# A fifth row buffer for gathered expert rows in the dense stage, and the Gelu of a dot issued a step later

## Chip, cores and metric

The kernel runs on one core of one Trainium2 chip. The metric is the device time of one execution in microseconds (us), median of the runs shown. Engines are named as the profile names them: PE (TensorE; PEld is its weight load), DVE (VectorE), ACT (ScalarE), POOL (GpSimd), SP (SyncE). POOL and SP do no arithmetic that matters here: they issue transfers.

## What is computed

The kernel is one layer of a hybrid network for 9 tiles of 128 tokens, each token a row of 1024 float32 values. A trunk (gated mixing, retention, projections) ends with scores for product-key retrieval. Each token then picks 8 heads x 16 = 128 experts out of 16384, and every expert is one row of `expert_u` and one of `expert_v`:

```python
experts = e1 * P_NKEYS + e2
w = jax.nn.softmax(vals, axis=-1).astype(t.dtype)
a = jax.nn.gelu(jnp.einsum('td,thkd->thk', t, eu[experts]))
return jnp.einsum('thk,thkd->td', w * a, ev[experts])
```

The result is added to the token's row and normalised.

## The kernel before, in words

**Two forms of the expert layer.** Token tiles 0, 1, 2, 6, 7 are *gathered*. For each of the 128 experts of a token, POOL issues one indirect transfer (L766) that brings, for the tile's 128 tokens, one row each of `euv` (2048 floats: u beside v, 128 x 8 KB = 1.05 MB) into a row buffer `gat`. DVE forms the dot of the u half with the token (L739, with a short read of its sum, `sdot`), ACT takes Gelu and multiplies by the softmax weight (L741, L742), and DVE adds the weighted v half to `acc` (L753). 5 x 128 = 640 such gathers are made. Tiles 3, 4, 5, 8 take the *dense* form: all 16384 experts in 128 steps of 128 experts. A step `e` forms `S` (24 matmuls, L988), ACT takes Gelu into `a` (L995), DVE multiplies by the spilled expert weights `pt` (L997), ACT and DVE split the product into two parts `g` (L200 cast, L204 subtract), and PE multiplies the parts with those of `ev` into `res` (18 matmuls) and `blk` (6 on average, L960), which DVE adds to `oacc` (L969).

**Weights of a dense step.** `fetch` (L937) loads 128 rows of u (`in_eud`) and of v (`in_evd`), 512 KB each, through four raw buffers `wraw`. `split_u` (L942) and `split_v` (L947) split them into two parts: an ACT cast (L200: `whi`, `ev`) and a DVE subtract (L204: `wlo`, `ev`). Every eighth step loads a 2 MB block of `pt`.

**Stages.** The trunk runs to about 2344 us with gathers beside it. Then comes the entry to the dense stage: the best keys and weights of tile 8 on DVE (L631 to L731), and their expansion into DRAM (`expand`, L772). The dense stage runs from 2494 to about 4111 us with the other gathers beside it, then the last norms.

**Order.** The program is written as generators: `advance` (L891) lets two lanes run, gathers and the preparation of expert weights, each yield counting modelled microseconds (a gather 5, one of a dense step's two halves 24 x 512 / 2400). A scheduler then places each engine's instructions by priority and by when it thinks their inputs are ready; dense work is issued at a raised priority (`DP`), and so is the preparation of the last tiles (`BOOST`). On the chip every engine takes its instructions in that fixed order, so an instruction that waits holds up all behind it on its engine.

**The pipeline of gathers** (L744): there are `GB = 4` row buffers. A gather is put on `queue`; the row issued `AHEAD = 2` steps ago is dotted and its Gelu issued at once; the row of the step before that is added, which frees its buffer. The transfer into a buffer can start when the add of the row four before is done.

```python
def gathered():
    if len(queue) > AHEAD and queue[AHEAD] is not None:
        dots(*queue[AHEAD])
    if len(queue) > AHEAD + LAG:
        last = queue.pop()
```

Of the kernel before, what the change touches and what calls it, by code (L numbers as in the profile page):

```python
# [17 lines left out]
P = 128  # L18
D = 1024
# [9 lines left out]

# units of the packed weights: [unit][128 rows of a k tile][4 k tiles][256 columns]  # L30
U_IN, U_PA, U_PB, U_OUT, U_Q, N_UNITS = 0, 80, 88, 104, 112, 128

# columns of the packed small vectors and constants
C_GMIX, C_GSGU, C_BG, C_GFFN, C_SK1, C_SK2 = 0, 8, 16, 32, 40, 168
N_VEC = 296
K_KDP, K_EPP, K_DMP, K_TRI, K_IOTA, K_ID = 0, 4, 8, 520, 648, 776
N_CST = 904
# the same for the sample tile
S_KDS, S_EPS, S_DMS, S_TRS = 0, 32, 36, 548
N_SMP = 676  # L40

GROUPS = [[0, 1], [2, 3, 4, 5], [6, 7, 8]]
# the token tiles whose experts' rows are gathered, and those that take the dense form
GATHER, DENSE = [0, 1, 2, 6, 7], [3, 4, 5, 8]
# those whose best keys are found next to the scores
EARLY = [0, 1, 8]
TD = len(DENSE) * P
EC = 4      # tokens in one product of their expert weights
LT = 16     # tokens in a run of the spilled expert weights
BE = 8      # second keys in one load of them  # L50

# [3 lines left out]
def step_kernel(ctx: ExitStack, tc: tile.TileContext, x, state, wall, wst, bs, rows, vec, cst, smp, cosd, sind, euv,  # L55
# [34 lines left out]

    # ---- weights: loaded ahead, split into two float32r parts whose sum is exact
    order = []
# [22 lines left out]
    def load(n):  # L115
        nonlocal pair
        if n < per - 2 and n % 3 < 2:
            # the slots of the gathered rows are free until the first token tiles are through
            if n % 3 == 0:
                pair = peer.tile([P, 2, 4, 256], F32, name="gat", bufs=GB)  # L120
            t = pair[:, n % 3]
        else:
            t = wp.tile([P, 4, 256], F32, name="wraw", bufs=NRAW)
        nc.sync.dma_start(t, wall[order[n]])
        return t

    def take():
        """the two parts of the weights of the next unit"""
        n = wst_["take"]
        wst_["take"] += 1  # L130
        while wst_["split"] < min(n + 3, len(order)):
            s = wst_["split"]
            while wst_["load"] < min(s + n_raw(wst_["load"]), len(order)):
                l = wst_["load"]
                raws[l] = load(l)
                wst_["load"] += 1
            hi, lo = (wp.tile([P, 4, 256], F32R, name=n, bufs=NPART) for n in ("whi", "wlo"))
            split((hi, lo), raws.pop(s))
            parts[s] = (hi, lo)
            wst_["split"] += 1  # L140
        return order[n], parts.pop(n)
# [6 lines left out]
    def store(out, src, after=2):  # L148
        """a store of something just computed: issued later, so that its wait holds up no load"""
        late.append([after, out, src])  # L150
# [11 lines left out]
    def col(t, k, T):  # L162
        """the k-th 128 rows of transposed activations: one tile, or one of every two"""
        return t[k // 2][:, k % 2, :T] if isinstance(t, list) else t[:, k, :T]

    def gemm_f(acts, T, base, nk=2):
        """columns of the weights on the partitions: [128, 2, T]"""
        ps = gp.tile([P, 2, 512], F32, name="gps")
# [12 lines left out]
    def gemm_t(acts, nt, base):  # L181
        """tokens on the partitions: [128, nt, 256]"""
        ps = gp.tile([P, 4, 256], F32, name="gps")
# [13 lines left out]
    def split(parts, src, scale=None):  # L197
        """parts[0] = float32r(src * scale), parts[1] = src * scale - parts[0]"""
        if scale is None:
            nc.scalar.copy(parts[0], src)  # L200
        else:
            nc.scalar.activation(parts[0], src, AF.Copy, scale=scale)
        if scale is None:
            nc.vector.tensor_tensor(parts[1], src, parts[0].bitcast(F32), op=OP.subtract)  # L204
        else:
            nc.vector.scalar_tensor_tensor(parts[1], src, scale, parts[0].bitcast(F32), op0=OP.mult, op1=OP.subtract)
# [11 lines left out]

    # ---- trunk of one group of token tiles, up to the sub-key scores
    hTs = {}  # L220

    def front(gi, pl):
        """the first norm of a group, transposed"""
        tl = GROUPS[gi]
# [217 lines left out]
    def gating(pl, tl, nt, T, sample, hT, pb):  # L442
        # of every two channel groups, the normalised v and then the high parts of their products
        va = []
# [94 lines left out]
    def project(pl, tl, nt, T, mT, tT, rs):  # L539
        """x + m @ w_out; the products with w_query start from it times g_ffn, their scores take the norm's factor"""  # L540
        grow = pl.tile([P, D], F32, name="grow")
# [74 lines left out]

    # ---- product-key retrieval
    AHEAD, LAG = 2, 1
    PACE = [5.0]
    BOOST = [100]  # L620
    AB = 2
    EUB, RWB = 3, 4
    AA = (1, 3)
# [15 lines left out]
    def top_keys(t, h, src):  # L639
        """the 16 best keys of each half of a head"""  # L640
        if t not in early:
# [10 lines left out]
    def topk_units(kind, t):  # L652
        """the experts of a token tile and their softmax weights"""
        d = T_[t] = {}
# [18 lines left out]
        v12, i12 = early.pop(t)  # L673
        # pairs (i, j) that may be among the 16 largest sums: (i + 1)(j + 1) <= 16, in the order of 16 i + j,
        # with a few more that make the rows regular
        cand = peer.tile([P, PH, 64], F32, name="cand", tag="oh")
# [59 lines left out]

    def dots(t, j, b):
        d = T_[t]
        nc.vector.tensor_tensor_reduce(out=b[:, :D], in0=b[:, :D], in1=d["x"], op0=OP.mult, op1=OP.add,  # L739
                                       scale=1.0, scalar=0.0, accum_out=d["s"][:, j:j + 1])  # L740
        nc.scalar.activation(d["s"][:, j:j + 1], d["s"][:, j:j + 1], AF.Gelu_apprx_tanh)  # L741
        nc.scalar.activation(d["s"][:, j:j + 1], d["s"][:, j:j + 1], AF.Copy, scale=d["w"][:, j:j + 1])  # L742

    def gathered():  # L744
        """one step of the pipeline gather -> dot -> accumulate"""
        if len(queue) > AHEAD and queue[AHEAD] is not None:
            dots(*queue[AHEAD])
        if len(queue) > AHEAD + LAG:
            last = queue.pop()
            if last is not None:  # L750
                t, j, b = last
                d = T_[t]
                nc.vector.scalar_tensor_tensor(d["acc"], b[:, D:], d["s"][:, j:j + 1], d["acc"], op0=OP.mult, op1=OP.add)  # L753
                if j == HK - 1:
                    out_norm(d["acc"], peer.tile([P, 2 * D], F32, name="gat", bufs=GB), t)
                    del T_[t]

    def gather(t):
# [5 lines left out]
        for j in range(HK):  # L764
            b = peer.tile([P, 2 * D], F32, name="gat", bufs=GB)
            nc.gpsimd.indirect_dma_start(out=b, out_offset=None, in_=euv,  # L766
# [5 lines left out]
    def expand(t):  # L772
        """the softmax weights of a token tile over all experts: [first key, second key, token], into DRAM"""
        d = T_.pop(t)
# [25 lines left out]
        for c in range(P // EC):  # L800
# [9 lines left out]
            for j in range(EC):  # L810
# [4 lines left out]
                else:  # L815
                    # max(0, w - w (n - e)^2) is w at n = e and 0 elsewhere
                    nc.scalar.activation(ab[:, 0, j], io, AF.Square, scale=-1.0, bias=eT[:, 0, k:k + 1])
# [8 lines left out]
    def out_norm(acc, tmp, t):  # L826
        """the last norm; tmp takes the squares and the norm's weights"""
        nc.sync.dma_start(tmp[:, D:], row_bcast(rows, 2))
        final_norm(acc, tmp[:, :D], tmp[:, D:], t)
# [10 lines left out]
    def prepare():  # L840
        """the top-k of all tiles, and the weights of the dense ones"""
        left, wait = list(GATHER), list(DENSE)
# [15 lines left out]
    def gather_all():  # L858
        for t in GATHER:
            while t not in staged:  # L860
                if any(queue):
                    queue.insert(0, None)
# [3 lines left out]
            yield from gather(t)  # L866
        for _ in range(AHEAD + LAG + 1):
            queue.insert(0, None)
# [35 lines left out]

    # ---- the dense form: every expert for the token tiles of DENSE
    prep = ExitStack()
# [72 lines left out]
    for e in range(NKEYS + 1):  # L979
        if e < NKEYS:  # L980
# [8 lines left out]
            del eu[e]  # L989
            split_v(e)  # L990
            fetch("ev", e + 1)
            fetch("eu", e + 2)
            split_u(e + 2)
            a = dp.tile([P, TD], F32, name="a", bufs=2)
# [3 lines left out]
            G[e] = [dp.tile([P, TD], F32R, name=f"g{m}", bufs=NBK + 1) for m in range(2)]  # L998
            split(G[e], a)
            hp.close()  # L1000
            advance(us)
# [67 lines left out]
def units(w):  # L1069
    """[rows, cols] -> [cols / 256][rows / 512][128][4 * 256]"""  # L1070
    r, c = w.shape
# [43 lines left out]
```

## Time and profile before

| what | value |
|---|---|
| three runs | 4148.25, 4151.52, 4161.88 us; median 4151.52 |
| profiled execution: span from first to last instruction | 4134.5 us |
| the runs' times above that span | 13.8 to 27.4 us, median 17.0 |
| busy share of the span: PE, DVE, ACT, POOL | 89%, 84%, 45%, 23% |
| transfers: mean rate over the span | 285 GB/s |
| dense stage, first `S` matmul to last | 2494.0 to 4111.1 us |
| gathers in the dense stage | 342 of 640 |

The profile shows the span of the profiled execution; its own time with what lies around the span is not shown apart from the three runs. A busy share is an average: three engines and the transfers are each near nine tenths in the dense stage, so what counts there is which of them makes the others wait, and when. Matmuls overlap, so PE's throughput is read from the number of matmuls in a stretch rather than from its busy time.

### The profile page before, as it was taken

What the parts mean: (1) busy time and instruction counts of PE and PEld (TensorE: products, weight loads), DVE (VectorE), ACT (ScalarE), POOL (GpSimd) and SP (SyncE); (2) the same over time, 40 slices, a digit from 0 to 9 for tenths busy, and PEclk for the clock granted to TensorE, in tenths of its full rate; (3) what the DMA queues carried; (4) which work ended last, traced back from release to release, by engine and by line L of the source; (5) the groups of instructions that cost most, each with busy time, mean ns of one, the idle gap of its engine ahead of it and who ended that gap; (6) DMA issues with size and microseconds to landing.
All of it is one profiled execution on the core that took longest, in us unless ns stands there. A gap on an engine that the chain in (4) does not pass through costs nothing.

```text
span 4134.5 us, 54954 instructions
## 1 busy us (share of the span) xinstructions
PE 3692.4 (89%) x19724; PEld 3100.0 (75%) x19724; DVE 3458.4 (84%) x6439; ACT 1844.7 (45%) x3879; POOL 948.1 (23%) x740
## 2 busy tenths in 40 slices
PE   8999999898988878998898748999999999899998
PEld 6779987786877777887898746777777777677776
DVE  5556699888888779989898888888998988888888
ACT  4445544434343533766666564333333333333333
POOL 0110002323322220121312212322122333233232
PEclk9999999999999988999999868999999999999999
DMA  7665547888888974675868847889778999889997
GB/s 281 214 217 189 209 151 288 340 311 334 336 308 331 335 270 140 209 278 193 297 213 313 308 132 273 332 337 343 274 290 338 354 341 346 327 341 339 342 338 285
DMA packets 247601, 1178.13 MB, mean 285 GB/s; under 512 B 28448, under 2 KB 47648, under 8 KB 163360
## 3 DMA queue, kind: packets, MB, share of 16 engines
q0 software_dynamic: 105984, 721.47, 47.3%
q1 hardware_dynamic: 141344, 453.16, 30.2%
q8 instruction: 155, 2.54, 0.2%
q14 instruction: 118, 0.97, 0.1%
HBM read 1096.92 MB, written 77.59 MB: 284 GB/s over the span
## 4 chain that ended last, share of the span: by engine, by line
issue 38%; PE 17%; DVE 15%; POOL 15%; DMA 11%; ACT 3%; POOLq 0%; SPq 0%; DVEq 0%; ACTq 0%
POOL gat L766 15%; PE gps L176 6%; PE gps L192 5%; DMA gat<-in_euv_dram,idx 3%; DMA pdr<-st 3%; DVE acc L753 2%; DVE wlo L204 2%; DVE gat L739 2%; PE sps L397 1%; PE sps L395 1%; PE S L988 1%; DMA wraw<-in_eud_dram 1%; DVE ktmp L633 1%; ACT st L794 1%; DMA s<-ssp 1%
## 5 line engine op out<-in xcount | busy, mean ns | idle before, releaser
L766 POOL DMA_INDIRECT gat<-in_euv_dram,idx x640 | 874.4, 1366 | 2695.7 <-DVE acc L753 1875.4
L739 DVE CUSTOM_DVE_ANT_0 gat<-gat,tx 128x1024 f32<-128x1024 f32 x640 | 779.5, 1218 | 266.9 <-DMA gat<-in_euv_dram,idx 260.0
L960 PE MATMUL res<-ev,g 128*128 128x512 f32 x2304 | 826.6, 402 | 79.7 <-ACT g L200 75.9
L753 DVE SCALAR_TENSOR_TENSOR acc<-gat,sdot,acc 128x1024 f32<-128x1024 f32 x640 | 817.7, 1278 | 16.0 <-ACT sdot L742 14.9
L988 PE MATMUL S<-h,whi 128*128 128x512 f32 x2048 | 776.2, 405 | 20.3 <-ACT a L995 16.2
L192 PE MATMUL gps<-whi,h 128*128 128x256 f32 x3456 | 655.1, 288 | 17.4 <-DVE rot L302 10.3
L741 ACT ACTIVATE sdot<-sdot 128x1 f32<-128x1 f32 x640 | 128.4, 202 | 1110.2 <-DVE sdot L739 1109.2
L960 PEld LDWEIGHTS res<-ev,g 128*128 128x128 f32 x2304 | 441.0, 193 | 206.7 <-ACT g L200 99.9
L192 PEld LDWEIGHTS gps<-whi,h 128*128 128x128 f32 x3456 | 551.7, 194 | 41.4 <-issue 31.4
L204 DVE TENSOR_TENSOR wlo<-wraw,whi 128x1024 fp32r<-128x1024 f32 x428 | 520.7, 1217 | 61.4 <-ACT whi L200 60.6
L200 ACT CAST whi<-wraw 128x1024 fp32r<-128x1024 f32 x428 | 446.0, 1044 | 269.9 <-PE gps L176 91.8
L192 PE MATMUL gps<-wlo,h 128*128 128x256 f32 x1728 | 496.4, 287 | 4.3 <-DVE wlo L204 4.3
L176 PE MATMUL gps<-h,whi 128*128 128x256 f32 (+2 forms) x1920 | 496.6, 341 | 0.9 <-ACT pb L328 0.6
L988 PEld LDWEIGHTS S<-h,whi 128*128 128x128 f32 x2048 | 395.9, 193 | 133.0 <-ACT a L995 47.6
L176 PE MATMUL gps<-y,whi 128*128 128x256 f32 (+2 forms) x1536 | 407.0, 347 | 27.9 <-ACT y L200 6.2
L988 PE MATMUL S<-h,wlo 128*128 128x512 f32 x1024 | 408.8, 399 | 0.0
L176 PEld LDWEIGHTS gps<-h,whi 128*128 128x128 f32 x1920 | 341.9, 191 | 28.2 <-ACT pb L328 1.0
L192 PEld LDWEIGHTS gps<-wlo,h 128*128 128x128 f32 x1728 | 335.6, 194 | 16.1 <-issue 10.7
L176 PE MATMUL gps<-h,wlo 128*128 128x256 f32 (+2 forms) x960 | 325.8, 339 | 0.4 <-DVE wlo L204 0.4
L176 PEld LDWEIGHTS gps<-y,whi 128*128 128x128 f32 x1536 | 276.3, 193 | 55.8 <-ACT y L200 6.9
L960 PE MATMUL blk<-ev,g 128*128 128x512 f32 x768 | 241.6, 407 | 41.5 <-DVE oacc L969 36.7
L176 PE MATMUL gps<-y,wlo 128*128 128x256 f32 (+2 forms) x768 | 263.3, 343 | 0.0
(217 smaller groups left out, 5204.9 us busy)
## 6 DMA issues: line engine op xcount, KB each, us to landing
wraw<-in_wall_dram SPq DMA_DIRECT2D x300, 512.0 KB
wraw<-in_eud_dram SPq DMA_DIRECT2D x128, 512.0 KB
wraw<-in_evd_dram SPq DMA_DIRECT2D x128, 512.0 KB
gat<-in_wall_dram SPq DMA_DIRECT2D x84, 512.0 KB
pdr<-st POOLq DMA_DIRECT2D x32, 1024.0 KB
pt<-pdr SPq DMA_DIRECT2D x16, 2048.0 KB
Sb<-in_state_dram SPq DMA_DIRECT2D x64, 256.0 KB
out_dram<-Sb POOLq DMA_DIRECT2D x64, 256.0 KB
```

The source lines that it names most:

```text
L176: mm(ps[:, c, :T], x, y, start=kh == 0 and k == 0 and j == 0, stop=kh == nk - 1 and k == 3 and j == len(pr) - 1)
L192: mm(ps[:, i], y, x, start=kh == 0 and k == 0 and j == 0 and i % 2 == 0, stop=kh == 1 and k == 3 and j == len(pr) - 1 and last)
L200: nc.scalar.copy(parts[0], src)
L204: nc.vector.tensor_tensor(parts[1], src, parts[0].bitcast(F32), op=OP.subtract)
L395: mm(pu, x, y, start=j == 0, stop=j == 2)
L397: mm(po[r:r + 2 * LS], qm[:, c, b], Sb, start=False, stop=b % 2 == 1 and c == 1)
L739: nc.vector.tensor_tensor_reduce(out=b[:, :D], in0=b[:, :D], in1=d["x"], op0=OP.mult, op1=OP.add, scale=1.0, scalar=0.0, accum_out=d["s"][ ...
L741: nc.scalar.activation(d["s"][:, j:j + 1], d["s"][:, j:j + 1], AF.Gelu_apprx_tanh)
L753: nc.vector.scalar_tensor_tensor(d["acc"], b[:, D:], d["s"][:, j:j + 1], d["acc"], op0=OP.mult, op1=OP.add)
L766: nc.gpsimd.indirect_dma_start(out=b, out_offset=None, in_=euv, in_offset=bass.IndirectOffsetOnAxis(ap=d["idx"][:, j:j + 1], axis=0))
L960: mm(ps, x, y, start=start and i == 0, stop=stop and i == 2)
L988: mm(ps, x, y, start=k == 0 and i == 0, stop=k == KD - 1 and i == 2)
```

## The change

Five things change (line numbers of the new kernel where they differ).

1. `dots` is parted into `dot` and `weigh`, and the dotted rows wait in a list. A step first issues the Gelu and weighting of the row that the step before dotted, then the dot of the next, then the add of the former. In program order Gelu moves from just behind its dot to the next step.
2. The lead of a gather over its dot, `AHEAD`, becomes a variable: 2 as before, and 3 from dense step 2 to step 124 of the program as written.
3. In the same stretch every fifth row goes into a further buffer `gats`, so five rotate.
4. Its memory comes from the split u weights: `EUB` goes from 3 to 2 buffers of `whi` and `wlo`.
5. In a dense step `split_v(e)` and `split_u(e + 2)` are written behind the split of `g` rather than ahead of the Gelu.

```diff
-    EUB, RWB = 3, 4
+    EUB, RWB = 2, 4
...
-    def dots(t, j, b):
+    def dot(t, j, b):
         d = T_[t]
         nc.vector.tensor_tensor_reduce(out=b[:, :D], in0=b[:, :D], in1=d["x"], op0=OP.mult, op1=OP.add,
                                        scale=1.0, scalar=0.0, accum_out=d["s"][:, j:j + 1])
+
+    def weigh(t, j, b):
+        d = T_[t]
         nc.scalar.activation(d["s"][:, j:j + 1], d["s"][:, j:j + 1], AF.Gelu_apprx_tanh)
         nc.scalar.activation(d["s"][:, j:j + 1], d["s"][:, j:j + 1], AF.Copy, scale=d["w"][:, j:j + 1])
...
     def gathered():
+        last = list(dotted)
+        dotted.clear()
+        for cur in last:
+            weigh(*cur)
+        while len(queue) > AHEAD[0]:
+            cur = queue.pop()
+            if cur:
+                dot(*cur)
+                dotted.append(cur)
+        for cur in last:
+            add(*cur)
+
+    spare = []
+
+    def row_buffer(j):
+        if spare and j % (GB + 1) == GB:
+            return spare[0].tile([P, 2 * D], F32, name="gats", bufs=1)
+        return peer.tile([P, 2 * D], F32, name="gat", bufs=GB)
...
             del eu[e]
-            split_v(e)
             fetch("ev", e + 1)
             fetch("eu", e + 2)
-            split_u(e + 2)
             a = dp.tile([P, TD], F32, name="a", bufs=2)
...
             split(G[e], a)
+            split_v(e)
+            split_u(e + 2)
+            if e == 2:
+                spare.append(dp)
+                AHEAD[0] = 3
+            if e == NKEYS - 4:
+                spare.clear()
+                AHEAD[0] = 2
```

**What this does to the order.** The trunk's order is nearly the same. Three places move.

*DVE at the entry to the dense stage*, where tile 8's experts are found (`vals`, `pos`, `ktmp`, `wp`, `pf`, `sh`). Before, dots (`ISA gat,sdot`) and adds (`acc`) stand between these:

```order
L753 SCALAR_TENSOR_TENSOR acc<-gat,sdot,acc 128x1024
L634 MAX vals<-ktmp 128x8
L739 ISA gat,sdot<-gat,tx 128x1024
L739 ISA sdot 128x1
L635 MAX_INDEX pos<-vals,ktmp 128x8
L728 TENSOR_TENSOR wp<-vals 128x128
L698 CAST pf<-pos 128x128
L699 TENSOR_SCALAR sh<-pos 128x128
```

After, the same place has none:

```order
L633 MATCH_REPLACE ktmp<-vals,cand 128x64
L634 MAX vals<-ktmp 128x8
L635 MAX_INDEX pos<-vals,ktmp 128x8
L728 TENSOR_TENSOR wp<-vals 128x128
L698 CAST pf<-pos 128x128
L699 TENSOR_SCALAR sh<-pos 128x128
L700 TENSOR_SCALAR fi<-sh 128x128
```

Ahead of the first multiply of a dense step (`a<-a,pt`) there stand 298 adds before and 280 after; between the first and the last of the 128 multiplies 342 and 343; behind the last 0 and 17.

*DVE at the end.* Before, the last rows are the norms of the dense tiles (`dx`) and of the last gathered tile:

```order
L1031 TENSOR_TENSOR dx_34327<-dx_34327,oacc31_22787 128x512
L835 SCALAR_TENSOR_TENSOR dx_34325<-dx_34325,rfin_34345,grow_34323 128x1024
L214 RECIPROCAL rfin_34354<-rfin_34354 128x1
L835 SCALAR_TENSOR_TENSOR dx_34326<-dx_34326,rfin_34354,grow_34323 128x1024
L214 RECIPROCAL rfin_34363<-rfin_34363 128x1
L835 SCALAR_TENSOR_TENSOR dx_34327<-dx_34327,rfin_34363,grow_34323 128x1024
L214 RECIPROCAL rfin_34998<-rfin_34998 128x1
L835 SCALAR_TENSOR_TENSOR acc_33322<-acc_33322,rfin_34998,gat_34996 128x1024
```

After, 14 dots and 15 adds follow the last `dx` addition (the first few shown), and only then the last tile's norm:

```order
L1057 TENSOR_TENSOR dx_34325<-dx_34325,oacc31_22785 128x512
L855 SCALAR_TENSOR_TENSOR dx_34324<-dx_34324,rfin_34352,grow_34321 128x1024
L739 ISA gat_34901,sdot_27867<-gat_34901,tx_33314 128x1024
L739 ISA sdot_27867 128x1
L214 RECIPROCAL rfin_34361<-rfin_34361 128x1
L749 SCALAR_TENSOR_TENSOR acc_33316<-gat_34895,sdot_27867,acc_33316 128x1024
L855 SCALAR_TENSOR_TENSOR dx_34325<-dx_34325,rfin_34361,grow_34321 128x1024
L739 ISA gat_34907,sdot_27867<-gat_34907,tx_33314 128x1024
```

*ACT in a dense step* (step 60; the numbers rise in the order in which the program is written). Before:

```order
L995 ACTIVATE a_28433<-S_28392 128x512
L200 CAST whi_28515<-wraw_28513 128x1024
L200 CAST g0_28436<-a_28433 128x512
L741 ACTIVATE sdot_22740<-sdot_22740 128x1
L742 ACTIVATE sdot_22740<-sdot_22740,wg_22741 128x1
```

After:

```order
L1013 ACTIVATE a_28415<-S_28386 128x512
L200 CAST whi_28430<-wraw_28413 128x1024
L744 ACTIVATE sdot_22738<-sdot_22738 128x1
L745 ACTIVATE sdot_22738<-sdot_22738,wg_22739 128x1
L200 CAST g0_28418<-a_28415 128x512
```

`whi` is now written behind `g0` in the program, but the scheduler still places it ahead. It is the split for step e + 3 before and for step e + 2 after. Over all 128 steps `whi` stands between `a` and `g0` on ACT in 121 steps before and 125 after; on DVE `wlo` stands ahead of the `g` subtract in 71 and 104 steps, a part of `ev` in 56 and 40. In 116 steps before and 113 after, exactly the Gelus of those dots stand ahead of `g0` on ACT that stand ahead of the same step's `a` multiply on DVE, so Gelu's place among the dots is the same.

POOL's order ends before with 342 gathers into `gat`; after, the last `gats` is used in dense step 94, and the order ends with `L786 DMA gat<-in_euv_dram,idx 128x2048 x113`.

## Rows read from the trace of the kernel before

**Rows 1.** The page: busy tenths in 40 slices of the span.
```profile
PE   8999999898988878998898748999999999899998
DVE  5556699888888779989898888888998988888888
DMA  7665547888888974675868847889778999889997
```

**Rows 2.** Windows: us, PE, PEld, DVE, ACT, POOL busy (xinstructions), PEclk, DMA share, GB/s.
```profile
2344.00:2410.00 66.00, 11.30 (x53) 9.20 (x51) 59.97 (x196) 16.33 (x39) 14.04 (x9) 0.57 0.73 263
2410.00:2494.00 84.00, 51.34 (x256) 47.73 (x256) 65.02 (x263) 75.29 (x170) 9.17 (x8) 0.68 0.36 103
2494.00:3690.00 1196.00, 1092.06 (x4501) 852.66 (x4502) 1040.51 (x1606) 430.34 (x980) 330.94 (x248) 0.97 0.87 327
3690.00:4111.00 421.00, 389.17 (x1608) 305.50 (x1607) 366.80 (x489) 149.63 (x358) 123.72 (x95) 0.96 0.89 331
```

**Rows 3.** Windows of the S matmuls alone (L988): us, PE, PEld, PEclk, DMA, GB/s.
```profile
2494.00:3690.00 1196.00, 771.10 (x2268) 431.42 (x2269) 0.97 0.87 327
3690.00:4111.00 421.00, 277.99 (x804) 152.92 (x804) 0.96 0.89 331
```

**Rows 4.** Two short windows, columns as in rows 2.
```profile
3200.00:3210.00 10.00, 10.00 (x46) 8.29 (x45) 9.57 (x14) 3.78 (x9) 2.82 (x2) 1.00 1.00 415
...
3309.00:3315.00 6.00, 4.63 (x21) 3.34 (x19) 0.47 (x1) 1.53 (x2) 0.94 (x1) 1.00 0.99 422
```

**Rows 5.** Waits of DVE, PE and ACT, 2520 to 3690: us in total, times, longest.
```profile
DVE gat L739 <- DMA gat<-in_euv_dram,idx: 111.3, 55, 5.9
...
PE res L960 <- ACT g L200: 50.2, 26, 4.8
PE blk L960 <- DVE oacc L969: 31.7, 25, 4.8
...
ACT sdot L741 <- DVE sdot L739: 443.7, 171, 5.5
...
ACT whi L200 <- DMA wraw<-in_eud_dram: 54.7, 14, 7.2
```

**Rows 6.** Timeline: a late row, start, us, instruction [idle before <-releaser].
```profile
2764.72 1.23 DVE L739 CUSTOM_DVE_ANT_0 gat<-gat,tx 128x1024 f32<-128x1024 f32 x1 [2.40 <-DMA gat<-in_euv_dram,idx]
...
2765.88 0.69 DVE L997 TENSOR_TENSOR a<-a,pt 128x512 f32<-128x512 f32 x1
...
2767.27 0.50 PE L960 MATMUL res<-ev,g 128*128 128x512 f32 x1 [1.33 <-ACT g L200]
```

**Rows 7.** Timeline: a late row and a late weight load.
```profile
3115.57 1.23 DVE L739 CUSTOM_DVE_ANT_0 gat<-gat,tx 128x1024 f32<-128x1024 f32 x1 [4.58 <-DMA gat<-in_euv_dram,idx]
...
3116.98 1.04 ACT L200 CAST whi<-wraw 128x1024 fp32r<-128x1024 f32 x1 [7.17 <-DMA wraw<-in_eud_dram]
...
3118.60 0.79 PE L960 MATMUL res<-ev,g 128*128 128x512 f32 x1 [4.76 <-ACT g L200]
```

**Rows 8.** Groups by line, DVE, 2344 to 2410: busy us, mean ns | idle before.
```profile
L753 DVE SCALAR_TENSOR_TENSOR acc<-gat,sdot,acc 128x1024 f32<-128x1024 f32 x9 | 11.5, 1275 | 0.5 <-ACT sdot L742 0.5
L739 DVE CUSTOM_DVE_ANT_0 gat<-gat,tx 128x1024 f32<-128x1024 f32 x9 | 10.9, 1209 | 1.1 <-DMA gat<-in_euv_dram,idx 1.1
```

**Rows 9.** Timeline near the end, DVE: a dot and the next, one add between.
```profile
4098.32 1.22 DVE L739 CUSTOM_DVE_ANT_0 gat<-gat,tx 128x1024 f32<-128x1024 f32 x1
...
4100.71 1.23 DVE L739 CUSTOM_DVE_ANT_0 gat<-gat,tx 128x1024 f32<-128x1024 f32 x1
```

**Rows 10.** Timeline of the end: dense tiles' last norm, then the last gathered tile's.
```profile
4127.33 1.06 ACT L833 ACTIVATE gat<-acc 128x1024 f32<-128x1024 f32 x1
...
4127.65 1.28 DVE L835 SCALAR_TENSOR_TENSOR dx<-dx,rfin,grow 128x1024 f32<-128x1024 f32 x1
...
4129.04 1.28 DVE L835 SCALAR_TENSOR_TENSOR acc<-acc,rfin,gat 128x1024 f32<-128x1024 f32 x1
4130.35 0.33 SPq L836 DMA_DIRECT2D out_dram<-acc  x1
```

More of the change, by code (lines that the diff above doesn't have):

```diff
@@ L615, in query @@
             pass
-    AHEAD, LAG = 2, 1
+    AHEAD = [2]
     PACE = [5.0]
@@ L740, in dots, with add @@
                                        scale=1.0, scalar=0.0, accum_out=d["s"][:, j:j + 1])
+    def weigh(t, j, b):
+        d = T_[t]
         nc.scalar.activation(d["s"][:, j:j + 1], d["s"][:, j:j + 1], AF.Gelu_apprx_tanh)
         nc.scalar.activation(d["s"][:, j:j + 1], d["s"][:, j:j + 1], AF.Copy, scale=d["w"][:, j:j + 1])
-    def gathered():
[L746 to L756, printed above, removed]
+    def add(t, j, b):
+        d = T_[t]
+        nc.vector.scalar_tensor_tensor(d["acc"], b[:, D:], d["s"][:, j:j + 1], d["acc"], op0=OP.mult, op1=OP.add)
+        if j == HK - 1:
+            out_norm(d["acc"], peer.tile([P, 2 * D], F32, name="gat", bufs=GB), t)
+            del T_[t]
+    dotted = []
+    def gathered():
+        last = list(dotted)
[14 more added lines that the diff above has]
+        return peer.tile([P, 2 * D], F32, name="gat", bufs=GB)
     def gather(t):
@@ L764, in gather @@
         for j in range(HK):
-            b = peer.tile([P, 2 * D], F32, name="gat", bufs=GB)
+            b = row_buffer(j)
             nc.gpsimd.indirect_dma_start(out=b, out_offset=None, in_=euv,
@@ L860, in gather_all @@
             while t not in staged:
-                if any(queue):
+                if any(queue) or dotted:
                     queue.insert(0, None)
@@ L866, in gather_all @@
             yield from gather(t)
-        for _ in range(AHEAD + LAG + 1):
+        while any(queue) or dotted:
             queue.insert(0, None)
```

## The prediction

> **What bounds the kernel now.** I read the slices of the page first, then the windows by stage, then the waits of the dense stage, then single stalls in the timeline. The slices [rows 1] show no idle engine to win from: from the entry to the dense stage on, PE, DVE and the transfers all stand at eight or nine tenths. The windows [rows 2, 3] give the stage its price per step. In 2494 to 3690 there are 2268 S matmuls, 24 to a step, so 94.5 steps of 12.66 us; in the last 421 us 33.5 steps of 12.57 us. A step has 48 matmuls, and a window in which PE never stops holds 46 in 10 us at full clock [rows 4], so PE alone would take about 10.6 us. Two microseconds of each step are lost on PE, to stalls and to the granted clock, which is 0.97 and 0.96 on average [rows 2].
>
> The waits say where from [rows 5]. In 2520 to 3690 DVE waits 55 times, 111.3 us in all, for a gathered row. PE waits 50.2 us for `g` and 31.7 us for `oacc`, both made behind those dots. One stall shows the chain [rows 6]: the dot stands ahead of the `a` multiply on DVE, starts 2.40 us late, and PE's first `res` matmul is 1.33 us late. So about 1.1 us of a DVE delay is slack. A second kind [rows 7] has two late inputs: the row comes 4.58 us late, the next u weights 7.17 us late, and since `whi` stands ahead of `g` on ACT, PE loses 4.76 us. Weights were late 14 times in that stretch [rows 5].
>
> **The change part by part.**
>
> *Gelu a step later: 0 us.* ACT waits 443.7 us for dots [rows 5], which would look like the prize. But ACT's order shows Gelu in the same place among the dots as before, and ACT is busy 430 of 1196 us [rows 2]. What could hurt is `g` behind a Gelu, and that relation did not move.
>
> *The entry: -23 us.* In 2344 to 2410 PE is busy 11.3 of 66 us and DVE 60.0 [rows 2]: DVE sets the time. Nine dots and nine adds lie there [rows 8], and after the change none. From one dot to the next with an add between takes 2.39 us [rows 9]; nine of these are 21.5 us, with the 1.6 us idle ahead of them [rows 8] 23. The other nine of the 18 adds that leave stand where PE is full, or beside the expansion in 2410 to 2494, where ACT is busy 75.3 of 84 us [rows 2], or in the first steps; I take nothing for them. Bounds: 24 at most (22.4 busy and 1.6 idle), 10 if the loads of the tokens become what is late.
>
> *The end: +42 us.* The 18 are not gone. 14 dots and 15 adds now stand behind the dense tiles' last addition, with nothing left to hide them. Before, DVE ends the dense norms at 4128.9 and the last gathered tile is through at 4130.3 [rows 10]. Four rows lie ready in the buffers: 4 x 2.39 = 9.6 us. The other ten need a transfer each. They cannot go faster than DVE, 2.39 us, and the dense stage's own pace is 421 / 95 = 4.43 us with weights beside it [rows 2]. A row tile of 1.05 MB at the best rate shown, 422 GB/s [rows 4], takes 2.5 us; I take 3.0, near that row, as the weights are gone: 30 us. Then one add (1.2), Square to final multiply (4127.33 to 4130.32, 3.0 us) and the last store to the span's end (4130.3 to 4134.5, 4.2 us) [rows 10]. 4128.9 + 9.6 + 30 + 1.2 + 3.0 + 4.2 = 4176.9, against 4134.5: +42. Bounds +36 (all at 2.39) and +57 (ten at 4.43).
>
> *The fifth buffer: -44 us.* The dense stage does as many adds as before, so per step nothing is added. With four buffers a transfer must land within the two dot-add rounds that follow the freeing add and the gap to its own dot; five give one round more, 1196 / 248 = 4.8 us on average [rows 2]. The mean wait is 111.3 / 55 = 2.0 us [rows 5], so most waits are shorter than what is added. Against it stands the rate: in the longest wait the transfers were already at 0.99 and 422 GB/s [rows 4], and a buffer brings no bandwidth. It only lets a row be fetched earlier, from the 13% of the stretch in which the transfers are not busy (155 us of 1196) [rows 2]. I take half of the waits as gone. Half of PE's 81.9 us [rows 5] is 41; half of what the clock costs (3% of 1196, 36 us) [rows 2] is 18; of the 59 I take off a quarter (14 of 55), since there late weights hold `g` back anyway [rows 5, 7]. That leaves 44. Bounds: 0, and 118 (81.9 + 36). The last 33 steps have no fifth buffer in POOL's order and keep their 12.57 us.
>
> *The splits: +2 us.* On ACT `whi` stays ahead of `g`, so a late weight load holds `g` as before. On DVE `wlo` (1.2 us) stands ahead of `g` in 33 more steps and a part of `ev` (0.6 us) in 16 fewer: at most 33 x 1.2 = 40 and less 16 x 0.6, 30 us, if all showed on PE. But ACT's cast of `g` runs at that time, and 1.1 us of delay is slack [rows 6], so I take 2. Two instead of three u buffers cost nothing: `whi` follows `a` on ACT and needs only the matmuls that `a` needed, and a whole step of PE lies between it and its use. If that cover went, each late weight load would stall the next S too; that price is in the second rival.
>
> The sum: -23 + 42 - 44 + 2 = -23 us on the span, 4134.5 to 4111.5. The median of the runs lies 17 us above that span, and I add the same: 4128.5, rounded 4128.
>
> **The rivals.** *The transfers are the bound (slower).* If the waits are there because the 16 transfer engines are full and not because rows are asked for late, the fifth buffer changes nothing: 4151.5 - 23 + 42 + 2 = 4172. For it: the share of 0.87 to 0.89 [rows 2] and the full rate in the longest wait [rows 4]. Against it: those waits come in bursts with idle transfers between. It decides once the stage gains less than 9 us, where the sum passes +12.
>
> *Rows against weights.* A fourth transfer in flight beside the weights can make them later. If each of the 14 late loads [rows 5] comes one row tile (2.5 us) later, ACT and PE lose 35 us: 4128 + 35 = 4163. The Trainium skill (Trainium Kernel Development and Optimization, Key Constraints) says that transfers issued from SP, ACT and POOL "all run on the same 16 DMA engines and interleave", by which this would be so. The trace agrees that far: in [rows 7] a row and a weight load are late together.
>
> *The buffer just pays for the tail.* With 20 us instead of 44 the sum is about +1: 4152.
>
> *Nearly all waits go.* DVE would then set the pace, at 1040.5 busy of 1196 us [rows 2]; with four fifths of the 118, 95 us: 4151.5 - 23 + 42 - 95 + 2 = 4077.
>
> That the change does not do what it says holds for Gelu and for the order of the splits, by the order alone; for the buffer it holds for a quarter of the steps.
>
> **How the numbers follow.** A measurement of this kernel tells a difference of 0.3%, 12.5 us, from none. My forecast has 0.42 (its own range 4100 to 4139, faster), nearly all waits gone 0.12 (faster), the buffer just paying 0.22 (same), the transfers as bound 0.16 (slower), rows against weights 0.08, half of it same and half slower. Faster 0.54, same 0.26, slower 0.20. The range leaves a tenth at each end. Low: the entry as taken, the end at its bound of 36 and 89 us from the buffer, -23 + 36 - 89 + 2 = -74, gives 4077. High: no gain in the stage and the end at 47 gives 4151.5 - 23 + 47 + 2 = 4178.
>
> **What would show it.** Right: the first S matmul at about 2471 instead of 2494; DVE's wait for rows in the first 94 steps about 55 us instead of 111, steps of about 12.2 us there and of 12.6 in the last 33; 14 dots with PE idle at the end, some 2.4 to 3 us apart, over about 45 us. Wrong in the term of the buffer if the waits stay near 111 us with transfers at 0.9; by the second rival if `whi` waits much over 55 us for its weights; wrong at the end if the tail's dots come over 4 us apart.

## The result, and the profile after

The changed kernel takes 4059.59 us (median of four runs, 4055.21 to 4061.48) against 4149.89 us before (four runs); the ratio is 0.9779, 95% interval 0.9759 to 0.9799. The prediction was 4128 us with a range of 4077 to 4178: the direction was right, but the gain was 90 us instead of 23, and the time lies below the range.

Every profiled run of this study lies about 2 us above its own span (the changed kernel 4061.48 and 4059.4). So the profiled execution of before, span 4134.5, was itself a short one: it stands for some 4136.5 us, below each of the timed runs of before. The experiment without the fifth buffer (below; its time is that of before, 4156.6 us, span 4156.3) is the better yardstick, and the table has both.

| us | first S matmul at | first to last S | last S to end | span | median |
|---|---|---|---|---|---|
| before | 2494.0 | 1617.1 | 23.4 | 4134.5 | 4149.9 |
| without the fifth buffer (x1) | 2502.0 | 1631.2 | 23.1 | 4156.3 | 4156.6 |
| the changed kernel | 2475.6 | 1506.4 | 77.4 | 4059.4 | 4059.6 |

Against x1 the change brings -26 at the entry, -125 in the dense stage and +54 at the end; against the profiled execution of before -18, -111 and +54.

The page, slices of the span, after (compare [rows 1]):

```profile
PE   8999999989989878989989858999999999999993
DVE  5556699888888779989888888999999999888887
DMA  8665637898989975585777836999969999998987
```

From slice 26 on PE now stands at nine tenths and DVE at eight or nine, but for the last slice: PE's 3 there is the tail, the rows that are left at the end. Windows of the changed kernel: the stretch with the fifth buffer, the stretch without, the end; columns as in [rows 2].

```profile
2475.60:3570.00 1094.40, 1060.38 (x4542) 848.19 (x4542) 1039.81 (x1598) 431.11 (x983) 362.66 (x249) 0.99 0.93 358
3570.00:3982.00 412.00, 379.99 (x1566) 294.65 (x1567) 357.88 (x477) 147.43 (x348) 125.25 (x95) 0.98 0.90 333
3982.00:4059.40 77.40, 10.47 (x38) 7.36 (x36) 55.67 (x74) 20.36 (x53) 20.12 (x14) 0.58 0.75 279
```

The same for the S matmuls alone, columns as in [rows 3]:

```profile
2475.60:3570.00 1094.40, 766.88 (x2292) 428.74 (x2292) 0.99 0.93 358
3570.00:3982.00 412.00, 267.63 (x779) 147.12 (x780) 0.98 0.90 333
```

2292 matmuls are 95.5 steps of 11.46 us, where before had 12.66 [rows 3]; 779 are 32.5 steps of 12.69 us, where before had 12.57. The gain stops where the fifth buffer stops. The rate went from 327 to 358 GB/s, with the same bytes per step and row.

Waits of the changed kernel from 2500 to 3570: us in total, times, longest (compare [rows 5]).

```profile
POOL gat L786 <- DVE acc L749: 500.8, 184, 20.8
...
POOL gats L786 <- DVE acc L749: 123.2, 46, 18.3
...
ACT ev L200 <- DMA wraw<-in_evd_dram: 18.2, 7, 4.0
...
ACT whi L200 <- DMA wraw<-in_eud_dram: 8.5, 5, 4.9
PE res L980 <- ACT g L200: 8.1, 8, 2.5
...
DVE gat L739 <- DMA gat<-in_euv_dram,idx: 5.4, 5, 2.2
...
PE blk L980 <- DVE oacc L989: 2.6, 3, 1.5
...
DVE gats L739 <- DMA gats<-in_euv_dram,idx: 1.0, 1, 1.0
```

DVE's wait for rows is 6.4 us (5.4 and 1.0) instead of 111.3, PE's for `g` and `oacc` 10.7 instead of 81.9. The same view of the last stretch, 3570 to 3982, four buffers again:

```profile
DVE gat L739 <- DMA gat<-in_euv_dram,idx: 46.0, 25, 3.5
...
PE blk L980 <- DVE oacc L989: 14.0, 12, 2.6
PE res L980 <- ACT g L200: 13.5, 11, 2.4
```

### The profile page after: what moved, and what is told of

Same layout as the page of the kernel before. It is cut to its first block, busy times and chain, and to the rows that moved or that the text cites. A ratio compares the mean times of both kernels' runs of the same rounds, so it can differ in the third digit from the quotient of the medians.

```text
span 4059.4 us, 55000 instructions
## 1 busy us (share of the span) xinstructions
PE 3655.6 (90%) x19724; PEld 3088.0 (76%) x19724; DVE 3459.1 (85%) x6439; ACT 1846.8 (45%) x3879; POOL 980.0 (24%) x740
## 4 chain that ended last, share of the span: by engine, by line
issue 31%; PE 24%; DVE 17%; POOL 13%; DMA 12%; ACT 3%; POOLq 0%; SPq 0%; ACTq 0%; DVEq 0%
POOL gat L786 12%; PE gps L176 6%; PE S L1008 5%; PE gps L192 4%; PE res L980 4%; DMA gat<-in_euv_dram,idx 3%; DMA pdr<-st 3%; DVE wlo L204 3%; DVE acc L749 2%; DMA wraw<-in_evd_dram 2%; DVE gat L739 1%; PE sps L397 1%; DMA s<-ssp 1%; PE sps L395 1%; PE blk L980 1%
## 5 line engine op out<-in xcount | busy, mean ns | idle before, releaser
L786 POOL DMA_INDIRECT gat<-in_euv_dram,idx x591 | 834.8, 1413 | 2409.6 <-DVE acc L749 1629.5
L739 DVE CUSTOM_DVE_ANT_0 gat<-gat,tx 128x1024 f32<-128x1024 f32 x591 | 719.7, 1218 | 173.7 <-DMA gat<-in_euv_dram,idx 158.4
L980 PE MATMUL res<-ev,g 128*128 128x512 f32 x2304 | 812.3, 395 | 24.1 <-ACT g L200 21.1
L1008 PE MATMUL S<-h,whi 128*128 128x512 f32 x2048 | 766.5, 401 | 30.1 <-ACT a L1013 26.0
L749 DVE SCALAR_TENSOR_TENSOR acc<-gat,sdot,acc 128x1024 f32<-128x1024 f32 x591 | 755.3, 1278 | 22.0 <-ACT sdot L745 21.2
L192 PEld LDWEIGHTS gps<-wlo,h 128*128 128x128 f32 x1728 | 336.9, 195 | 16.2 <-issue 10.7
L200 ACT CAST ev<-wraw 128x512 fp32r<-128x512 f32 x256 | 158.0, 621 | 236.2 <-PE res L980 103.3
```

The lines of the kernel that those rows point to most:

```text
L192: mm(ps[:, i], y, x, start=kh == 0 and k == 0 and j == 0 and i % 2 == 0, stop=kh == 1 and k == 3 and j == len(pr) - 1 and last)
L980: mm(ps, x, y, start=start and i == 0, stop=stop and i == 2)
L1008: mm(ps, x, y, start=k == 0 and i == 0, stop=k == KD - 1 and i == 2)
```

## The experiments

The theory: the gain is the fifth buffer's alone. With four, a row's transfer starts so late that it often lands after DVE's turn to dot it; `a`, `g` and PE follow. Rivals: the splits' new place, the Gelu's, the longer lead. "Four" and "five" below mean row buffers in the dense stage. All ratios are against the kernel before, timed on the same chip.

### One part without the others

x1, the change without the buffer and the lead:

```diff
-            if e == 2:
-                spare.append(dp)
-                AHEAD[0] = 3
-            if e == NKEYS - 4:
-                spare.clear()
-                AHEAD[0] = 2
```

> The changed kernel without its fifth row buffer and without the longer lead; Gelu a step later, two buffers of split u weights and the splits behind g stay. Theory (the buffer gives the gain): about as before, 4140 to 4160 us, with DVE waiting 100 to 120 us for gathered rows in the first 94 dense steps, steps of 12.5 to 12.7 us, 298 adds ahead of the dense stage and none behind it. Rival (the splits' new place gives the gain, and with it the late weight loads vanish): 4060 to 4085 us, waits for u weights in ACT near 9 us instead of 55.

Measured: 4156.59 us, ratio 1.0001 (0.9984 to 1.0017). Its S matmuls, and its waits in the first 1094 us of the stage but 20:

```profile
2502.00:3596.40 1094.40, 700.13 (x2064) 393.70 (x2064) 0.96 0.87 324
```

```profile
POOL gat L786 <- DVE acc L749: 700.0, 204, 18.5
...
DVE gat L739 <- DMA gat<-in_euv_dram,idx: 113.6, 50, 6.5
...
PE blk L980 <- DVE oacc L989: 45.6, 23, 6.1
PE res L980 <- ACT g L200: 34.8, 22, 3.9
ACT whi L200 <- DMA wraw<-in_eud_dram: 7.6, 2, 5.2
...
ACT ev L200 <- DMA wraw<-in_evd_dram: 5.0, 2, 2.7
```

Steps of 12.73 us, and rows late for 113.6 us. Half of the rival came true and paid nothing: the late loads of u weights are gone (7.6 us), with the time of before. x1 has the splits' new place and two u buffers together; no run has the new place with three.

x2, the kernel before with the Gelu a step later and nothing else (`dots` parted into `dot`, `weigh` and `add` as in the change; `EUB` 3, splits ahead of the Gelu of the dense step, no `spare`).

> The kernel before with the Gelu of a dot written a step later, and nothing else of the change. Theory: no difference, 4145 to 4155 us, since Gelu stands in the same place among the dots. Rival (Gelu's place gives a part): under 4138 us, with ACT's wait for dots (443.7 us in 2520 to 3690 before) well down.

Measured: 4158.72 us, ratio 1.0009 (0.9988 to 1.0029): no difference, though 4 us above the range given. x5 puts the Gelu back and keeps the rest:

```diff
-        for cur in last:
-            weigh(*cur)
...
                 dot(*cur)
+                weigh(*cur)
```

> The changed kernel with the Gelu of a dot issued right behind its dot again; all else of the change stays. Theory (Gelu's place is worth nothing): 4050 to 4070 us, like the changed kernel. Rival (with five buffers the later Gelu frees ACT, which then no longer holds g): 4075 us or more, with PE's wait for g well over 8 us in the first 94 dense steps.

Measured: 4064.4 us, ratio 0.9772 (0.9745 to 0.98), as the changed kernel. Gelu's place is worth nothing from either side. In x2 `whi` was late again, as before the change:

```profile
DVE gat L739 <- DMA gat<-in_euv_dram,idx: 99.9, 47, 6.0
...
ACT whi L200 <- DMA wraw<-in_eud_dram: 54.3, 13, 7.5
...
PE res L980 <- ACT g L200: 47.8, 22, 5.1
...
PE blk L980 <- DVE oacc L989: 32.7, 25, 5.0
```

x1 differs from x2 in the splits' place and the number of u buffers. The two have 7.6 and 54.3 us of late u weights, and the same time within 0.3%; PE waits 80.4 and 80.5 us for `g` and `oacc` together.

x4, the buffer without the longer lead:

```diff
             if e == 2:
                 spare.append(dp)
-                AHEAD[0] = 3
```

> The changed kernel with the lead of a gather over its dot kept at two steps; five buffers rotate. Theory (the buffer, by the earlier start of a transfer, gives the gain; which step of the program the dot is written in matters little as the scheduler places it): 4055 to 4075 us, waits of DVE for rows under 30 us in the first 94 dense steps. Rival (the longer lead in the program gives it, the buffer alone does not): 4120 us or more, with waits for rows near 100 us.

Measured: 4046.14 us, ratio 0.9744 (0.9727 to 0.976), with 1490.4 us from first to last S and 6.1 us of waits for rows in its first 1094 us. That is 9 us below the range given. The buffer does all of it without the longer lead; the lead of three may cost some 10 us, but the two intervals just touch, and this was not followed further.

x3, the splits written ahead of the Gelu again, with two buffers of split u weights:

```diff
             del eu[e]
+            split_v(e)
             fetch("ev", e + 1)
             fetch("eu", e + 2)
+            split_u(e + 2)
...
             split(G[e], a)
-            split_v(e)
-            split_u(e + 2)
```

> The changed kernel with split_v and split_u written ahead of the Gelu as before; the buffer, the lead and two buffers of split u weights stay. In its order all 640 adds end within the dense stage, 360 between the first and the last multiply, none behind. Theory (the buffer gives the gain): the dense stage keeps most of the gain per step but must hold 17 adds more, and the tail of 54 us goes: 4010 to 4060 us. Rival (the splits' place gives the gain): 4130 to 4160 us.

Measured: 4086.37 us, ratio 0.9834 (0.981 to 0.9859): above the range given, though no tail is left (23.2 us from the last S to the end). The stage takes 1579.8 us, 73 more than the changed kernel's; 17 more rows at 2.39 us [rows 9] explain 41 at most, so at least 32 are left. A new wait stands in its first 1094 us, which the changed kernel does not have:

```profile
ACT whi L200 <- PE S L1008: 71.0, 40, 4.0
```

With two buffers the split for step e + 2 must wait until S of step e has read its weights, and here it stands ahead of what PE needs next. The late loads of u weights are gone here too (0.4 us in the same view), with the splits in their old place, so the new place is not what it takes for that. The new place with two buffers gains nothing (x1), but in the old place two buffers bring this wait. That the 32 us are its price is likely and not shown: DVE also waits longer for rows in x3 than in the changed kernel (34.4 us against 6.4).

### What makes a row late

x7 keeps four buffers and parts each 2 MB load of `pt` into four, a block ahead, since the longest wait for a row in x1, 6.5 us, came some 13 us behind the issue of such a load:

```diff
+            if e % 2 == 0 and e // BE + 1 < NKEYS // BE:
+                q, n = e % BE // 2, TD // LT // 4
+                nc.sync.dma_start(ptn.rearrange("p c e t -> p c (e t)")[:, q * n:q * n + n],
+                                  pdr[e // BE + 1][:, q * n:q * n + n])
```

> The run without a fifth buffer (4157 us), with each 2 MB load of expert weights parted into four of 512 KB, one every second step, a block ahead. Theory (rows are late behind bursts of other transfers, and the fifth buffer's longer lead rides these out): waits for rows fall from 114 to some 50 to 70 us in the first 1094 us of the stage, and the time to 4080 to 4125 us. Rival (rows are late at all times because four buffers give too little lead, bursts or not): waits for rows stay above 95 us, time 4140 us or more.

Measured: 4174.39 us, ratio 1.0052 (1.0032 to 1.0071). The longest wait fell from 6.5 to 4.3 us, but there are more:

```profile
DVE gat L739 <- DMA gat<-in_euv_dram,idx: 108.1, 66, 4.3
```

The bursts of `pt` are not the cause; my theory for this run falls, and its rival holds.

x12 keeps four buffers and halves the bytes of a gather; it leaves the v half out, so it does not compute the layer and serves for the time alone:

```diff
-            nc.gpsimd.indirect_dma_start(out=b, out_offset=None, in_=euv,
+            n = D if half else 2 * D
+            nc.gpsimd.indirect_dma_start(out=b[:, :n], out_offset=None,
+                in_=euv.rearrange("r (h d) -> (r h) d", h=2) if half else euv,
```

> The run without a fifth buffer (4157 us), where from dense step 2 of the program on each gather brings rows of 1024 instead of 2048 floats (the first half of another row; the v half is left out, and the add takes the dot's products), so half the bytes from the same number of rows and buffers. Theory A (a row is late because its transfer, of 1.05 MB, takes longer than four buffers leave it; shorter transfers cure it as a longer lead does): waits for rows fall from 114 us to under 30 in the first 1094 us of the stage, the steps go to 11.3 to 11.6 us, time 4000 to 4060 us (there is no tail here). Theory B (a fixed time from issue to landing is what four buffers do not cover, bytes or not): waits for rows stay above 70 us, time 4100 us or more.

Measured: 3998.6 us, ratio 0.9603 (0.9566 to 0.964). Its S matmuls and its waits, the same stretch as x1:

```profile
2509.30:3603.70 1094.40, 763.39 (x2290) 427.39 (x2291) 0.99 0.72 240
```

```profile
POOL gat L790 <- DVE acc L750: 640.2, 228, 20.9
...
DVE gat L739 <- DMA gat<-in_euv_dram,idx: 35.1, 24, 4.3
```

Waits for rows are 35.1 us, a little more than theory A said, the time is 1.4 us below its range, and the steps are 1094.4 / (2290 / 24) = 11.47 us: the step of five buffers with whole rows, 11.46, at 240 GB/s instead of 358. A shorter transfer and an earlier start do the same to the step. Half the bytes also leave the transfers less busy (0.72), so x12 by itself does not tell length from load; that load is not the bound shows in the changed kernel, whose transfers are busier than those of x1 (0.93 against 0.87) and whose rows are on time.

The traces of the changed kernel tell an earlier start from a faster transfer. Of the gathers into `gat`, from issue to landing, with five buffers (2500 to 3570), then with four (3570 to 3982):

```profile
DMA to landing us min/median/max: 3.5/8.6/14.1
...
DMA to landing us min/median/max: 5.7/7.9/13.0
```

With five buffers a transfer takes no less time; it is its start that is earlier. At 412 / 95 = 4.34 us a row, two rounds are 8.7 us and three 13.0, which is my estimate of what four and five buffers leave to a transfer: the median fits into either, the longest needs about three.

### The last third, and the rows at the end

x6 takes the lead of two and counts a gather as 3.4 instead of 5 modelled us from step 2 on, so that the program issues the last gathers sooner and the fifth buffer serves to the end of the stage:

```diff
-                AHEAD[0] = 3
+                PACE[0] = 3.4
```

> The run with a lead of two steps (4046 us), and from dense step 2 on a gather counts 3.4 instead of 5 modelled us, so that in program order the last gathers are issued earlier: the fifth buffer is used to the end of the dense stage (71 rows instead of 49) and 2 adds instead of 16 stand behind the dense tiles' last addition. Theory (each dense step with four buffers costs 1.1 us more than one with five, and each row in the tail 3 us): 33 steps x 1.1 = 36 us and up to 14 x 3 = 42 us less, while the 14 rows cost some 14 x 2.4 = 34 us of DVE within the stage if DVE is what bounds there: 3975 to 4015 us. Rival (the last steps are slow for another reason than the fourth buffer, as the last stretch of every kernel so far): 4030 us or more, with steps of 12.5 us in the last third.

Measured: 4004.86 us, ratio 0.9622 (0.9596 to 0.9648). S matmuls of its last third, then DVE's waits for rows there:

```profile
3576.30:3936.10 359.80, 259.80 (x768) 141.50 (x766) 1.00 0.97 374
```

```profile
DVE gat L739 <- DMA gat<-in_euv_dram,idx: 3.0, 2, 1.8
DVE gats L739 <- DMA gats<-in_euv_dram,idx: 0.5, 1, 0.5
```

768 matmuls are 32 steps of 11.24 us, against 12.69 in the changed kernel: the same steps, now with the fifth buffer. Most of the gain on the changed kernel is here, 32 x 1.45 = 46 of 55 us; the end is only 12 us shorter (65.6 us after the last S), since the rows that left the place behind the last dense addition now stand between the last multiply and that addition.

x8 adds x7's small loads to x6.

> The lead of two steps, gathers counted at 3.4 us from dense step 2 on, and the expert weights in loads of 512 KB: all together. Theory: what the small loads win with four buffers is mostly won by the fifth buffer already, so within 15 us of the run without the small loads, 3965 to 4015 us. Rival (the bursts cost with five buffers too): 20 us or more below that run.

Measured: 4005.91 us, ratio 0.9635 (0.9618 to 0.9652): nothing, as expected.

x9, x10 and x11 switch the fifth buffer on later, with the lead of two; x10 and x11 also count gathers at 3.4 us:

```diff
-            if e == 2:
+            if e == 12:
...
-                AHEAD[0] = 3
```

> The run with a lead of two steps (4046 us), with the fifth buffer switched on at dense step 12 of the program instead of 2; gathers count 5 modelled us again. In its order 299 adds stand ahead of the dense stage and none behind it, as before the change, and the fifth buffer is used to step 88. Theory (the 18 rows went from the entry to the end because of the early switch; they cost 54 us there and 18 to 27 us here, and each step with four buffers 1.1 us): first S matmul at about 2495 to 2503, 23 us from the last S to the end, 4046 + 25 - 54 + 10 to 15 = 4025 to 4035 us. Rival (the 18 rows at the end are no loss, since the rows cost their time wherever they stand): 4040 us or more.

> The same with gathers counted at 3.4 modelled us from step 12 on, so that the fifth buffer is used to step 125. Theory: 37 steps more with five buffers, 1.1 us each, 40 us below the run without: 3980 to 4000 us, with steps near 11.4 us in the last third and 23 us from the last S to the end. Rival (the gain of the last third came from the rows that were left to the tail, not from the buffer): 4015 us or more.

> The same switched on at step 10: 295 adds ahead of the dense stage, none behind. Theory: within 8 us of the run from step 12, since 4 rows more in the dense stage (some 2.4 us of DVE each) stand against 4 fewer at the entry. Rival (DVE is what bounds the stage with five buffers, so that each row moved into it costs more there than at the entry): 8 us or more above it.

Measured: x9 4043.49 us, ratio 0.974 (0.9704 to 0.9775); x10 4015.25 us, 0.9663 (0.9633 to 0.9692); x11 4003.37 us, 0.9633 (0.9603 to 0.9663). By stages, beside the runs they came from:

| us | first S at | first to last S | last S to end |
|---|---|---|---|
| x4 (lead of two, from step 2) | 2469.6 | 1490.4 | 76.9 |
| x9 (from step 12) | 2508.7 | 1510.4 | 23.9 |
| x6 (faster, from step 2) | 2481.9 | 1454.2 | 65.6 |
| x10 (faster, from step 12) | 2506.3 | 1483.4 | 25.7 |
| x11 (faster, from step 10) | 2510.8 | 1467.4 | 24.6 |

The early switch does send the 18 rows from the entry to the end. But x9 is a miss, and by its time the rival holds: the rows cost 39 us at the entry, and the stage lost 20 us where I had allowed 10 to 15, so it gains 3 us on x4, not 11 to 21. The 39 us stand between two single executions; over all profiles the first S comes at 2469.6 to 2483.1 us in the six with the early switch and at 2494.0 to 2510.8 in the eight others, 27 us apart on average. x10 comes out at the edge of its rival's range (4015 or more), but not for the rival's reason: it is x9 less 28 us, 27 of them in the stage, so the fifth buffer in the last third is worth something without any tail, if less than the 40 I expected. x11 is 12 us better than x10 where I expected 8 at most, of either sign. Why two steps of the switch are worth that was not tried.

x6, x8 and x11, at 4003 to 4006 us, beat the changed kernel by 54 to 56 us. x6 is the simplest: one line.

## Why the prediction was wrong in size

*Gelu a step later, 0 us.* Right: x2 and x5. The reading of the order, that Gelu stood in the same place among the dots, was enough, whatever the 443.7 us that ACT waits [rows 5] suggest.

*The entry, -23 us.* Right in mechanism and size: no dot and no add is left between 2344 us and the first S, and the gain is 18 us against the profiled execution of before, 26 against x1, 27 between the averages above.

*The end, +42 us.* Right in mechanism, 12 us short; measured +54, within its bounds of 36 and 57. DVE at the end of the changed kernel, start, us, instruction [idle before <-releaser]:

```profile
3992.60 0.69 DVE L1057 TENSOR_TENSOR dx<-dx,res 128x512 f32<-128x512 f32 x1 [5.11 <-DMA dx<-xsp]
...
4008.36 1.28 DVE L855 SCALAR_TENSOR_TENSOR dx<-dx,rfin,grow 128x1024 f32<-128x1024 f32 x1
...
4029.13 1.22 DVE L739 CUSTOM_DVE_ANT_0 gat<-gat,tx 128x1024 f32<-128x1024 f32 x1
...
4030.96 1.28 DVE L749 SCALAR_TENSOR_TENSOR acc<-gat,sdot,acc 128x1024 f32<-128x1024 f32 x1 [0.60 <-ACT sdot L745]
4032.16 1.22 DVE L739 CUSTOM_DVE_ANT_0 gat<-gat,tx 128x1024 f32<-128x1024 f32 x1
...
4054.18 1.29 DVE L855 SCALAR_TENSOR_TENSOR acc<-acc,rfin,gat 128x1024 f32<-128x1024 f32 x1
```

From the last S to the end of the dense norms (4009.6) it is 27.6 us, 9.8 more than before (4111.1 to 4128.9): DVE waits 5.11 us for a dense tile's tokens, and rows stand between the norms; this was not in the sum, and it is most of the 12. Each later row takes 3.03 us (4029.13 to 4032.16), which I had from the transfers' rate. The number is right and its reason wrong: the row is dotted and added at once, so DVE waits 0.60 us for Gelu and weighting, and the transfers are mostly on time.

*The splits, +2 us.* Too small to be seen (x1 is at 1.0001). But "a late weight load holds `g` as before" was wrong, since late u weights went from 54.7 us to 7.6 (x1), and "two instead of three u buffers cost nothing" is shown only with the splits behind `g`: in the old place `whi` waits 71.0 us for S (x3).

*The fifth buffer, -44 us.* **This is the step that failed.** Measured over the stage: -111 us against the profiled execution, -125 against x1; in the 95.5 steps that have it -115 and -121, by 12.66 and 12.73 us a step against 11.46. Its upper bound was 118. The bound's parts were right: against x1, PE's waits for `g` and `oacc` fell from 80.4 to 10.7 us and the granted clock rose from 0.96 to 0.99, some 33 us of 1094, together 103. Wrong were the two reductions, from 118 to 59 and from 59 to 44.

"I take half of the waits as gone", on the ground that the transfers stood at 0.99 and 422 GB/s in the longest wait, so that a buffer brings no bandwidth. One wait at the full rate was taken for the whole stretch, whose mean was 0.87 busy: with five buffers the transfers then held 374 GB/s at 0.97 for 360 us (x6), where four had 324 to 333. The text had the other half of the argument, a mean wait of 2.0 us against 4.8 us of added lead, and even the longest wait, 5.9 us, is little more than that. That half was right: a transfer takes no less time with five buffers (median 8.6 us against 7.9), and the rows are on time. A row of the trace of before, which the prediction does not use, says what starts a transfer:

```profile
POOL gat L766 <- DVE acc L753: 756.8, 226, 21.2
```

That is 2520 to 3690: POOL waited for a freed buffer before 226 of 242 gathers. When nearly every transfer starts at the moment a buffer comes free, a further buffer moves nearly every start. But this row alone does not tell late rows from punctual ones: with five buffers POOL still waits for nearly every gather (184 and 46 times for 247), and so it does in x12 (228 of 245). Whether the transfers had room for the earlier starts was open before the change; the changed kernel and x6 show that they had.

"Of the 59 I take off a quarter", because late weights hold `g` back anyway. They vanished already in x1, from 54.7 to 7.6 us, and nothing was gained. In such a stall two inputs are late together [rows 7], and curing one leaves the other to set the end; the change cured both, so there was nothing to take off. What five row buffers bring while u weights stay late no run shows.

The last 33 steps, forecast unchanged, were: 12.69 us against 12.57. The 10.6 us for PE alone are 10.4 by the row that they are taken from (48 matmuls at 46 in 10 us); the shortest steps measured are 11.24 us (x6).

*The 17 us around the span.* Wrong as named: around the span lie 2 us, and the other 15 are the distance of one short execution from the median. Carrying them over does no harm to the change itself, -23 us, which stands against the -90 us of the medians.

*The rivals.* "The transfers are the bound" falls with x6's rate. "Rows against weights" did not come: beside x1 the fifth buffer leaves u weights as they were (7.6 and 8.5 us); v weights got later, 5.0 us in x1 and 18.2 in the changed kernel, while PE's waits for `g` and `oacc` fell. The rule of the Trainium skill behind that rival (Trainium Kernel Development and Optimization, Key Constraints: transfers issued from SP, ACT and POOL share 16 engines and interleave) is not contradicted by this, but it says nothing about which load is needed when. "Nearly all waits go", given 0.12, was what happened; its 4077 us is still 17 above the measured time.

## What to carry to other kernels

To price one more buffer, compare the waits at the consumer with the lead that a buffer adds. Where they are shorter, where the issuing queue waits for a freed buffer nearly every time, and where the transfers have room over a long stretch (here 0.87), nearly all of those waits may go, with their followers on PE and the clock. This case shows it for one kernel. Test a bandwidth objection on a long stretch, not on one stall. Of two inputs that are late together, curing one can be worth nothing, as the weights were here (x1 against x2). And read a buffer's switch as a change of order as well. Here it moved 18 rows from the entry to the end, which saved some 26 us and cost 54; yet keeping them at the entry gained little (x9 against x4) or nothing (x11 against x6), since they cost their time there and in the stage. And the buffer was off for the last third, which cost some 36 us (x6 against x4).

## What was not expected of the hardware

With the same bytes per row and step, the transfers' rate in the dense stage rose from 324 GB/s (x1, 0.87 busy) to 358 (0.93); in the last third of x6, which has 2.9 rows to a step instead of 2.6, it was 374 GB/s (0.97). Meanwhile waits for rows fell from 113.6 us to 6.4 and, in that third, 3.5, though a single transfer took no less time from issue to landing (8.6 us against 7.9). And at 240 GB/s (x12, 0.72 busy) four buffers still left 35.1 us of late rows: a low mean share of the transfers did not mean that every row was on time.
